# Hybrid attention block: when the branch-weight sums and the pooling weights' high part are issued, and where three down products accumulate

## The chip, the cores and the metric

The kernel runs on one core of one Trainium2 chip. The metric is the device time of one execution in microseconds (us). Before the change the median of 3 runs is 1093.87 us (1093.35 to 1094.19).

## The reference, cut to what matters

One decoder layer on 1024 tokens of width 1024, all in float32 (cut):

```python
h = _rmsnorm(x, g_mix_pre[l])
proj = jnp.einsum('bsd,de->bse', h, w_in[l]) + b_in[l]
u_pool, q, k, v, gates = jnp.split(proj, IN_SPLITS, axis=-1)
y_pool = _multiscale_pool(u_pool, w_pool[l], pool_scale[l])   # 4 groups of 128 channels; w_pool, then * pool_scale
y_attn = _sliding_window_sink_attention(rope(q), rope(k), v, attn_sinks[l])   # 8 heads of 64, window 128, one sink each
g_pool, g_attn = jax.nn.sigmoid(gates)[..., :D_MODEL], jax.nn.sigmoid(gates)[..., D_MODEL:]
merged = (g_pool * jnp.einsum('bsc,cd->bsd', y_pool, w_branch_pool[l])
          + g_attn * jnp.einsum('bsc,cd->bsd', y_attn, w_branch_attn[l]))
x = x + _rmsnorm(jnp.einsum('bsd,de->bse', merged, w_out[l]), g_mix_post[l])
h2 = _rmsnorm(x, g_mlp_pre[l])
ff = jnp.einsum('bsf,fd->bsd',
                jnp.square(jax.nn.relu(jnp.einsum('bsd,df->bsf', h2, w_up[l]))), w_down[l])
x = x + _rmsnorm(ff, g_mlp_post[l])
```

## The kernel before

**Matmuls.** Each float32 operand is split into a high part (a cast, mostly on ScalarE, L101) and a low part (a subtraction, mostly on VectorE, L104), and each product takes three passes on TensorE (PE): high by high, high by low, low by high. The large products are of Strassen's kind, seven products of halves in place of eight, so that sums of weights are formed on VectorE before they are split.

**Attention.** This is the first 150 us or so. The tokens are eight tiles of 128. For a tile, `post_qkv` transposes queries and keys on PE (L345, L346) and splits them. `score_all` forms the scores (matmuls of L389, two groups, each in a PSUM bank tagged `sc`, of which there are two), and ScalarE copies each group to SBUF (L391). `score_prev` puts the previous tile's scores into the masked places on VectorE (L398). `softmax_max` (L405 to L407), `softmax_exp` (ScalarE, L413 for the sinks, then L415 for eight heads) and `softmax_scale` (VectorE: L419 adds the sink to the sum, L420 its reciprocal, L421 scales) follow. `attend_t` transposes the probabilities on PE (L432) and splits them (L101, L104), `attend_own` masks a copy of them (L441), and `attend_v` multiplies by the values on PE and copies the result, `yt`, on ScalarE (L459), out of an `sc` bank. GpSimd (POOL) does beside this the rotation of queries and keys of a tile (L326 to L329) and the copies, differences and splits of its values (L354, L103, L359, L104 with `v`, `dv`, `df`).

The order of PE, VectorE and ScalarE in this stage is written out by hand under `manual_schedule`: each engine issues its instructions in the order of the code. `fill(t)` puts some t us of other matmuls between the steps (L183 is one of their lines): first the query, key and value projections of tiles 4 to 7, closed on VectorE by L312 (queries) and L315 (keys and values), then gate products `half(p, i)` and the four pooling products `wb_mm(gi)`. What these need made ready on ScalarE and VectorE is kept in lists of closures, `between`, `due` and `lazy`, that are flushed at set places; `lazy` behind the scaling L421, or ahead of `wb_mm`.

**The branch sums.** `w_branch_attn` is loaded in two halves h (0 and 1), each into two tiles of the three-buffer pool `st` (tag `st`, `presum_load`, its DMAs at L276 on SP's queue). `presum(h)` is called twice for each: the first call does the sums L286 and L287, the second L282 and L283 and then stores four blocks. All are VectorE additions or subtractions of 128x512 with both operands in SBUF. The loads of half 1 are issued behind the split of the pool weights `wpt` (a ScalarE L101 and a VectorE L104), which also came through a buffer of `st`.

**The pooling weights.** `load_wb(gi)`, called in the stream of `fill` for gi = 3, 2, 1, 0, loads 512 KB of `w_branch_pool` into a buffer of `st` (DMA at L700) and appends one closure `parts`: ScalarE scales it into the high part (L705), VectorE forms the low part (L706). For gi of 3 and 2 it goes to `lazy`, for 1 and 0 to `between`.

**The down stage.** It begins behind the up products and takes the rest of the time. Seven products `PRODUCTS = (1, 5, 2, 3, 6, 7, 4)`, each of eight steps, each step loading and splitting a pair of operands and adding into four PSUM banks [128, 512], one for a tile of 128 tokens (`down_mm`, matmuls L1982). Banks have two tags, `at` and `mm`, of four each. Products 1 and 2 use one set of `at`, 5 and 3 one set of `mm`; 6 takes new `at` banks, 7 new `mm`, 4 new `at`. `u`, `v`, `c11`, `c12` are accumulators in SBUF, four tiles of [128, 512] each. Behind products 1 and 2 ScalarE copies the banks to `u` (L2097) and `c11` (L2101); behind 6, 7 and 4 VectorE adds the banks to `u`, `v` or `c12`. With product 4 the tokens 512 to 1023 are closed tile by tile: in `last_tile` the last six matmul passes of the last tile are done on the left 256 columns, then on the right 256 in a bank of their own, and VectorE adds each to `u` (L2046 whole, L2048 right); the squares, the root, one scaling of the whole `c11` and the output follow.

## Time and profile before

| | |
|---|---|
| median of 3 runs | 1093.87 us (1093.35 to 1094.19) |
| the profiled execution's own time | 1093.78 us |
| its span, first to last instruction | 1092.0 us |
| mean granted TensorE clock | 0.998 of full |
| PE, VectorE, ScalarE, POOL busy | 99%, 74%, 56%, 8% of the span |

All durations are of the one profiled execution; about 1.8 us of its time lies outside the span. In a row of the timeline stand the start, from the span's beginning, and the length in us, the engine (PE, DVE for VectorE, ACT for ScalarE, POOL, SPq for SP's queue of DMAs), the line of the kernel, the operation and its output and inputs; in square brackets the idle time ahead of it and what ended that. "x18" counts instructions that are shown together. A row of the busy times by stretch holds the stretch, its length, then the busy time and the count of instructions of PE, PEld (weight load), DVE, ACT and POOL, then the granted clock, the DMA engines' share and GB/s. A row of DMA transfers ends with the size of one and the median time from issue to landing.

### The profile page before, as it was taken

How to read it: one execution, taken by the hardware profiler on the slowest of the kernel's cores; microseconds unless marked ns; L12 is line 12 of the kernel's file. 1: busy time of each engine (PE TensorE's matmuls, PEld its weight loads, DVE VectorE, ACT ScalarE, POOL GpSimd, SP SyncE). 2: the span in 40 equal slices, each digit the busy share in tenths (PEclk: the TensorE clock that was granted, in tenths of full speed). 3: DMA queues.
4: the chain of work that ended last, by engine and by line, in shares of the span. 5: the costliest groups of instructions: out<-in, count | busy, mean ns of one | idle time of the engine just before them, and what ended most of it. 6: DMA issues, size and time to landing. Idle time of an engine off the chain costs nothing.

```text
span 1092.0 us, 13883 instructions
## 1 busy us (share of the span) xinstructions
PE 1082.5 (99%) x5066; PEld 899.1 (82%) x5066; DVE 810.4 (74%) x1111; ACT 610.8 (56%) x1001; POOL 84.2 (8%) x142
## 2 busy tenths in 40 slices
PE   9999999999999999999999999999999999999997
PEld 8888888888888888888888888888888888888886
DVE  6689888999797887889867665655457866557685
ACT  7557886466654257457665564555346535435461
POOL 0344311100100012100000000000000000000000
PEclk9999999999999999999999999999999999999999
DMA  9858899679865776732565535345697886632622
GB/s 337 189 142 212 212 247 349 189 242 319 255 214 173 225 182 154 270 117 81 180 212 212 193 125 191 127 161 186 223 389 278 298 261 194 195 117 78 212 77 77
DMA packets 98612, 221.02 MB, mean 202 GB/s; under 512 B 10224, under 2 KB 27760, under 8 KB 98544
## 3 DMA queue, kind: packets, MB, share of 16 engines
q1 hardware_dynamic: 82256, 183.56, 50.2%
q0 software_dynamic: 10528, 16.78, 8.6%
q10 hardware_dynamic: 5760, 19.79, 4.8%
q8 instruction: 39, 0.64, 0.2%
q14 instruction: 29, 0.24, 0.1%
HBM read 158.24 MB, written 60.82 MB: 201 GB/s over the span
## 4 chain that ended last, share of the span: by engine, by line
PE 95%; DVE 2%; ACT 2%; DMA 0%; issue 0%; DVEq 0%; ACTq 0%; SPq 0%
PE mm L584 26%; PE at L584 18%; PE at L1982 15%; PE mm L1982 12%; PE mm L1516 5%; PE mm L495 3%; PE sc L183 2%; PE at L1244 2%; PE at L1516 2%; PE mm L192 2%; PE mm L1244 1%; PE mm L183 1%; PE mm L497 1%; PE sc L457 1%; PE sc L389 1%; PE at L1562 1%
## 5 line engine op out<-in xcount | busy, mean ns | idle before, releaser
L1982 PE MATMUL at<-ar,wh 128*128 128x512 f32 x696 | 159.0, 389 | 0.0
L1982 PEld LDWEIGHTS at<-ar,wh 128*128 128x128 f32 x696 | 130.6, 188 | 27.5 <-DVE ar L104 0.4
L1982 PE MATMUL mm<-ar,wh 128*128 128x512 f32 x576 | 131.0, 389 | 0.0
L1982 PEld LDWEIGHTS mm<-ar,wh 128*128 128x128 f32 x576 | 108.1, 188 | 22.5
L104 DVE TENSOR_TENSOR wh<-raw,wh 128x1024 fp32r<-128x1024 f32 x50 | 61.1, 1223 | 68.4 <-ACT wh L101 68.2
L101 ACT CAST wh<-raw 128x1024 fp32r<-128x1024 f32 x50 | 52.6, 1052 | 104.0 <-PE at L1982 51.6
L104 DVE TENSOR_TENSOR wh<-st,wh 128x512 fp32r<-128x512 f32 (+1 forms) x103 | 74.8, 736 | 30.0 <-ACT wh L101 25.5
L584 PE MATMUL mm<-T,wx 128*128 128x512 f32 x375 | 90.4, 389 | 0.0
L584 PEld LDWEIGHTS mm<-T,wx 128*128 128x128 f32 x375 | 70.4, 188 | 14.6
L584 PE MATMUL mm<-gr,wh 128*128 128x512 f32 x321 | 77.2, 391 | 0.0
L101 ACT CAST wh<-st 128x512 fp32r<-128x512 f32 (+2 forms) x102 | 65.7, 653 | 19.3 <-PE at L584 5.6
L584 PEld LDWEIGHTS mm<-gr,wh 128*128 128x128 f32 x321 | 59.9, 188 | 12.2
L584 PE MATMUL mm<-T,wh 128*128 128x512 f32 x267 | 66.1, 389 | 0.0
L104 DVE TENSOR_TENSOR ar<-B,ar 128x1024 fp32r<-128x1024 f32 x43 | 52.5, 1220 | 9.8 <-ACT ar L101 9.4
L584 PE MATMUL at<-gr,wh 128*128 128x512 f32 x243 | 59.0, 389 | 0.0
L584 PE MATMUL mm<-x,wh 128*128 128x512 f32 x240 | 58.9, 394 | 0.0
L584 PEld LDWEIGHTS mm<-T,wh 128*128 128x128 f32 x267 | 50.1, 188 | 10.4
L584 PEld LDWEIGHTS at<-gr,wh 128*128 128x128 f32 x243 | 45.6, 188 | 9.5
L584 PEld LDWEIGHTS mm<-x,wh 128*128 128x128 f32 x240 | 44.2, 188 | 9.6 <-ACT f L693 0.2
L584 PE MATMUL at<-T,wx 128*128 128x512 f32 x213 | 52.0, 389 | 0.0
L101 ACT CAST ar<-B 128x1024 fp32r<-128x1024 f32 x43 | 45.1, 1050 | 12.2 <-DMA B<-in_w_dn_dram 9.4
L584 PEld LDWEIGHTS at<-T,wx 128*128 128x128 f32 x213 | 40.0, 188 | 8.3
(510 smaller groups left out, 2127.0 us busy)
## 6 DMA issues: line engine op xcount, KB each, us to landing
raw<-f_dram SPq DMA_DIRECT2D x52, 512.0 KB, 3.9
B<-in_w_dn_dram SPq DMA_DIRECT2D x32, 512.0 KB, 6.7
f_dram<-g SPq DMA_DIRECT2D x28, 512.0 KB, 3.3
st<-in_w_up_dram SPq DMA_DIRECT2D x24, 512.0 KB, 4.7
g<-spill_dram SPq DMA_DIRECT2D x17, 512.0 KB, 5.7
f_dram<-g ACTq DMA_DIRECT2D x17, 512.0 KB, 2.6
st<-in_w_g_dram SPq DMA_DIRECT2D x16, 512.0 KB, 4.9
g<-in_w_up_dram SPq DMA_DIRECT2D x15, 512.0 KB, 5.9
```

Of the source, the lines that this page charges most:

```text
L101: act.copy(hi, src)
L104: eng.tensor_tensor(lo, src, f32(hi), ALU.subtract)
L183: pe.matmul(bq, xs_[k][n // 4][:, xh, n % 4 * P:(n % 4 + 1) * P], wq[k][:, h, :], start=k == 0 and j == 0, stop=k == NK - 1 and j == 2)
L192: pe.matmul(bkv_of(n), xs_[k][n // 4][:, xh, n % 4 * P:(n % 4 + 1) * P], wkv[k // 2][:, h, k % 2, :], start=k == 0 and j == 0 and not (joi ...
L389: pe.matmul(sb[:, kv, i, :nk], qt[r, qx, m * P:(m + 1) * P], kx[r, k0:k0 + nk], start=j == 0, stop=j == 2)
L457: pe.matmul(yb[:, kv], v[:, c:c + P], p[ph][:, 4 * kv:4 * kv + 4].rearrange("p i q -> p (i q)"), start=j < 2, stop=j >= len(mms) - 2)
L495: pe.matmul(bs[th], whi[:, k, :], rhs(k, hl, th), start=k == 0 and hl == 0, stop=False)
L497: pe.matmul(bs[th], wlo[:, k, :], rhs(k, 0, th), start=False, stop=k == nk - 1)
L584: pe.matmul(b, w[wh][:, kt, :], x_, start=not after and kt == 0 and j == 0, stop=kt == 3 and j == 2, skip_group_check=after)
L1244: pe.matmul(b, w[wh][:, kt, :], xo[xh][:, kt, :], start=not after and kt == 0 and j == 0, stop=kt == 1 and j == 2, skip_group_check=after)
L1516: pe.matmul(bs[t], Am[a][k][ah][:, t * P:(t + 1) * P], Wm[w][k][wh], start=not after and k == 0 and j == 0, stop=k == 3 and j == 2, skip_g ...
L1982: pe.matmul(bs[t], fo[fh][:, k2, t * P:(t + 1) * P], wo_[wh][:, k2, :], start=not after and s2 == 0 and k2 == 0 and j == 0, stop=(s2, k2) ...
```

## The change

Four things are done; no matmul of the attention stage is moved.

1. `presum(0)`'s second call, with L282 and L283 and the four stores, goes from ahead of `softmax_scale(0)` to behind `post_qkv(1)`. Both calls of `presum(1)` go from behind `score_all(2)` and `softmax_max(2)` to behind `attend_t(0)`, which is ahead of `softmax_scale(1)`.
2. The pooling weights' parts become two closures. The one of the high part of gi 3 and 2 is put into a new list `eager`, which is flushed behind each `attend_t`, so ahead of the next tile's exponentials. The low part stays where it was.
3. In the down stage `u` is copied by ScalarE back into the `at` banks behind product 2, and products 6, 7 and 4 add to these. ScalarE copies the banks to `u` behind 6 and 7 for the sums with `c12` and `v`; the closing steps of product 4 read the banks. The squares and scaling of `c12` are issued behind step 0 of product 7.
4. `last_tile` does the right columns first; ScalarE copies the right half of the bank out and VectorE adds the right product to it (256 wide); the left half is read from the bank. `c11` is scaled in two halves.

```diff
@@ -667,7 +667,7 @@
     wu, wb = {}, {}
 
 
-    between, hurry, due, lazy = ([], []), [False], ([], []), []
+    between, hurry, due, lazy, eager = ([], []), [False], ([], []), [], []
 
     def flush(todo):
         while todo:
@@ -699,12 +699,19 @@
         ws = stage([D])
         nc.sync.dma_start(ws, w_bp[gi])
 
-        def parts():
-            hi, lo = wb[gi] = wslot([D]), wslot([D])
-            sc = vec[:, V_PS + gi:V_PS + gi + 1]
-            act.activation(hi, ws, AF.Identity, scale=sc)
-            dve.scalar_tensor_tensor(lo, ws, sc, f32(hi), ALU.mult, ALU.subtract)
-        (lazy if gi > 1 else between[0]).append(parts)
+        sc = vec[:, V_PS + gi:V_PS + gi + 1]
+
+        def high():
+            wb[gi] = wslot([D]), wslot([D])
+            act.activation(wb[gi][0], ws, AF.Identity, scale=sc)
+
+        def low():
+            if gi not in wb:
+                high()
+            dve.scalar_tensor_tensor(wb[gi][1], ws, sc, f32(wb[gi][0]), ALU.mult, ALU.subtract)
+        if gi > 1:
+            eager.append(lambda: gi in wb or high())
+        (lazy if gi > 1 else between[0]).append(low)
 
     def wb_mm(gi):
 
@@ -913,6 +920,7 @@
         softmax_max(0)
         fill(1.7)
         post_qkv(1)
+        presum(0)
         fill(0.7)
         softmax_exp(0, range(3))
         fill(2.5)
@@ -921,7 +929,6 @@
         score_prev(1, 0)
         score_prev(1, 1)
         fill(0.7)
-        presum(0)
         softmax_scale(0)
         post_qkv(2)
         softmax_max(1)
@@ -934,7 +941,11 @@
         fill(3.7)
         for n in range(NT):
             attend_t(n)
+            flush(eager)
             attend_own(n)
+            if n == 0:
+                presum(1)
+                presum(1)
             flush(due[0])
             if n + 1 < NT:
                 early = 1.0 if n > 2 else 0.0
@@ -961,8 +972,6 @@
             hurry[0] = False
             if n + 2 < NT:
                 score_all(n + 2)
-                if n == 0:
-                    presum(1)
                 score_prev(n + 2, 0)
                 score_prev(n + 2, 1)
             flush(due[1])
@@ -976,8 +985,6 @@
                 gt.load(17, yy.tile([P, NK, P], F32, tag="y", name="r17"))
             if n + 2 < NT:
                 softmax_max(n + 2)
-            if n == 0:
-                presum(1)
             if n:
                 attend_sum(n - 1)
         gt.sums56(8)
@@ -2035,23 +2042,27 @@
         t = n - 4
         sums = small(2, "sq")
         b2 = bank("mm", [256])
-        for h, o in ((0, b[:, :256]), (1, b2)):
-            c = slice(h * 256, (h + 1) * 256)
+        left, right = slice(0, 256), slice(256, 512)
+        for o, c in ((b2, right), (b[:, left], left)):
             for s2, k2, _ in order:
                 fo, wo_ = opers[i, s2]
                 for j, (fh, wh) in enumerate(PASSES):
                     pe.matmul(o, fo[fh][:, k2, t * P:(t + 1) * P], wo_[wh][:, k2, c],
-                              start=h == 1 and k2 == 0 and j == 0, stop=k2 == 1 and j == 2, skip_group_check=h == 0)
-            if h == 0:
-                dve.tensor_tensor(u[t], u[t], b, ALU.add)
+                              start=c is right and k2 == 0 and j == 0, stop=k2 == 1 and j == 2,
+                              skip_group_check=c is left)
+            if c is right:
+                r_ = u[t][:, c]
+                act.copy(r_, b[:, c])
+                dve.tensor_tensor(r_, r_, b2, ALU.add)
+                act.activation(junk[:, c], r_, AF.Square, scale=ROOT_D, accum_out=sums[:, 0:1])
+                dve.scalar_tensor_tensor(c11[t][:, c], r_, -0.5, gfin_b[:, c], ALU.mult, ALU.mult)
             else:
-                dve.tensor_tensor(u[t][:, c], u[t][:, c], b2, ALU.add)
-            act.activation(junk[:, c], u[t][:, c], AF.Square, scale=ROOT_D, accum_out=sums[:, h:h + 1])
+                act.activation(junk[:, c], o, AF.Square, scale=ROOT_D, accum_out=sums[:, 1:2])
         e = small()[:, :1]
         dve.tensor_tensor(e, sq[:, 1, n:n + 1], sums[:, 0:1], ALU.add)
         s, ms, r, t2 = (small()[:, :1] for _ in range(4))
         act.activation(s, sums[:, 1:2], AF.Sqrt, bias=e)
-        dve.scalar_tensor_tensor(c11[t], u[t], -0.5, gfin_b[:, :512], ALU.mult, ALU.mult)
+        dve.scalar_tensor_tensor(c11[t][:, left], b[:, left], -0.5, gfin_b[:, left], ALU.mult, ALU.mult)
         dve.tensor_tensor(ms, sums[:, 1:2], e, ALU.add)
         dve.reciprocal(r, s)
         dve.scalar_tensor_tensor(t2, r, r, ms, ALU.mult, ALU.mult)
@@ -2077,39 +2088,47 @@
     for j, (i, s_) in enumerate(steps):
         if j + AHEAD < len(steps):
             operands(*steps[j + AHEAD])
-        if s_ == 0 and i not in (2, 3):
-            tag = "mm" if i in (5, 7) else "at"
-            banks[i] = [bank(tag) for _ in range(4)]
-        bs = banks[{2: 1, 3: 5}.get(i, i)]
+        if s_ == 0 and i in (1, 5):
+            banks[i] = [bank("mm" if i == 5 else "at") for _ in range(4)]
+        bs = banks[{2: 1, 3: 5, 7: 6, 4: 6}.get(i, i)]
         if i == 5:
             square_x1(s_)
         if i == 7 and 1 <= s_ <= 4:
             fin_out(s_ - 1, (c11, c12))
         if i != 4 or s_ < NS - LATE:
-            down_mm(i, s_, bs, i in (2, 3), [(s_, k2, t) for k2 in range(2) for t in range(4)
+            down_mm(i, s_, bs, i not in (1, 5), [(s_, k2, t) for k2 in range(2) for t in range(4)
                                              if (i, s_, t) != (4, NS - LATE - 1, 3)])
+            if (i, s_) == (7, 0):
+                with tc.issue_after(copied.ins):
+                    for t in range(4):
+                        fin_sq(t, 1, c12[t])
+                for t in range(4):
+                    fin_gain(1, c12[t], c12[t])
+                add_eps(slice(0, 4), 1)
+                rsqrt_sum(rr[:, 0:4], sq[:, 0, 0:4], sq[:, 1, 0:4], 4)
             if s_ < NS - 1:
                 continue
         elif s_ < NS - 1:
             continue
+        if i in (1, 6, 7):
+            for t in range(4):
+                copied = act.copy(u[t], bs[t])
         for t in range(4):
             if i == 1:
-                act.copy(u[t], bs[t])
-            elif i == 5:
+                continue
+            if i == 5:
                 act.copy(v[t], bs[t])
             elif i == 2:
                 act.copy(c11[t], bs[t])
+                banks.setdefault(6, []).append(bank("at"))
+                act.copy(banks[6][t], u[t])
                 fin_half(t, 0, c11[t])
             elif i == 3:
                 act.copy(c12[t], bs[t])
             elif i == 6:
-                dve.tensor_tensor(u[t], u[t], bs[t], ALU.add)
                 dve.tensor_tensor(c12[t], c12[t], u[t], ALU.add)
+            elif i == 7:
                 dve.tensor_tensor(v[t], v[t], u[t], ALU.add)
-                fin_half(t, 1, c12[t])
-            elif i == 7:
-                dve.tensor_tensor(v[t], v[t], bs[t], ALU.add)
-                dve.tensor_tensor(u[t], u[t], bs[t], ALU.add)
                 fin_sq(4 + t, 1, v[t])
                 if t == 3:
                     dve.scalar_tensor_tensor(v[t], v[t], -0.5, gfin_b[:, 512:], ALU.mult, ALU.mult)
@@ -2119,15 +2138,14 @@
                 n = 4 + t
                 late = [(s2, k2, t2) for s2, t2 in LATE_ORDER[t] for k2 in range(2)]
                 if t == 3:
-                    down_mm(i, s_, bs, False, late[:-2], late[-3])
+                    down_mm(i, s_, bs, True, late[:-2], late[-3])
                     with tc.manual_schedule(engines={mybir.EngineType.PE, mybir.EngineType.DVE,
                                                      mybir.EngineType.Activation}):
                         last_tile(i, n, bs[t], late[-2:])
                     continue
-                down_mm(i, s_, bs, False, late)
-                dve.tensor_tensor(u[t], u[t], bs[t], ALU.add)
-                fin_sq(n, 0, u[t])
-                fin_gain(0, c11[t], u[t])
+                down_mm(i, s_, bs, True, late)
+                fin_sq(n, 0, bs[t])
+                fin_gain(0, c11[t], bs[t])
                 rsqrt_sum(rr[:, n:n + 1], sq[:, 0, n:n + 1], sq[:, 1, n:n + 1])
                 fin_out(n, (c11, v))
         if i == 2:
@@ -2136,9 +2154,6 @@
             add_eps(slice(4, NT), 1)
             for n in range(4, NT):
                 load_x1(n)
-        if i == 6:
-            add_eps(slice(0, 4), 1)
-            rsqrt_sum(rr[:, 0:4], sq[:, 0, 0:4], sq[:, 1, 0:4], 4)
```

VectorE's order at the first place, from the splits of tile 1 (`qt`, `klo`) to the first step of tile 0's softmax scaling (L419), before (a row holds the line, the operation, output and inputs by the program's names, and the output's size; `st` are the branch weights, `sc` the score banks, `mm` the projections' banks):

```order
L104 TENSOR_TENSOR qt_656<-mm_649,qt_656 128x512
L104 TENSOR_TENSOR klo_471<-mm_650,khi_470 128x128
L312 SCALAR_TENSOR_TENSOR qkv_689<-mm_597,r_86,bc_461 128x512
L398 COPY_PREDICATED s_103_697<-cst,sc_698 128x2x256
L398 COPY_PREDICATED s_103_697<-cst,sc_712 128x2x256
L282 TENSOR_TENSOR st_464<-st_465,st_464 128x512
L283 TENSOR_TENSOR st_465<-st_465,st_464 128x512
L419 TENSOR_TENSOR den_636<-den_636,es_635 128x8
```

The same place after the change:

```order
L104 TENSOR_TENSOR qt_656<-mm_649,qt_656 128x512
L104 TENSOR_TENSOR klo_471<-mm_650,khi_470 128x128
L282 TENSOR_TENSOR st_464<-st_465,st_464 128x512
L283 TENSOR_TENSOR st_465<-st_465,st_464 128x512
L312 SCALAR_TENSOR_TENSOR qkv_695<-mm_597,r_86,bc_461 128x512
L398 COPY_PREDICATED s_103_703<-cst,sc_704 128x2x256
L398 COPY_PREDICATED s_103_703<-cst,sc_718 128x2x256
L419 TENSOR_TENSOR den_636<-den_636,es_635 128x8
```

The pair L282, L283 has passed three instructions, and L419 follows L398 directly.

VectorE's order at the second place, from the split of tile 0's probabilities (L104 of `sc_822`) to the first L398 of tile 2, before:

```order
L104 TENSOR_TENSOR s_122_821<-sc_822,s_121_820 128x1024
L419 TENSOR_TENSOR den_774<-den_774,es_773 128x8
L420 RECIPROCAL den_774<-den_774 128x8
L421 TENSOR_TENSOR s_103_697<-s_103_697,den_774 128x1024
L312 SCALAR_TENSOR_TENSOR qkv_860<-mm_810,r_86,bc_461 128x512
L315 SCALAR_TENSOR_TENSOR qkv_860<-mm_862,r_86,bc_461 128x256
L286 TENSOR_TENSOR st_784<-st_783,st_784 128x512
L287 TENSOR_TENSOR st_783<-st_783 128x512
L398 COPY_PREDICATED s_130_906<-cst,sc_907 128x2x256
```

The same place after the change:

```order
L104 TENSOR_TENSOR s_122_821<-sc_822,s_121_820 128x1024
L286 TENSOR_TENSOR st_784<-st_783,st_784 128x512
L287 TENSOR_TENSOR st_783<-st_783 128x512
L282 TENSOR_TENSOR st_783<-st_784,st_783 128x512
L283 TENSOR_TENSOR st_784<-st_784,st_783 128x512
L419 TENSOR_TENSOR den_774<-den_774,es_773 128x8
L420 RECIPROCAL den_774<-den_774 128x8
L421 TENSOR_TENSOR s_103_703<-s_103_703,den_774 128x1024
L312 SCALAR_TENSOR_TENSOR qkv_868<-mm_810,r_86,bc_461 128x512
L315 SCALAR_TENSOR_TENSOR qkv_868<-mm_870,r_86,bc_461 128x256
L398 COPY_PREDICATED s_130_914<-cst,sc_915 128x2x256
```

All four sums of half 1 now stand ahead of tile 1's softmax scaling; before, two stood behind it and two behind tile 2's first maximum (L407).

ScalarE's order around the first pooling weights, from the cast of tile 2's probabilities (L101 of `sc_1162`) to the copy of its attention output (L459), before:

```order
L101 CAST s_175_1160<-sc_1162 128x1024
L413 ACTIVATE es_1153<-es_1153 128x8
L415 ACTIVATE s_159_1085,den_1154<-s_159_1085,nmx_1152 128x128 x8
L705 ACTIVATE wh_1189<-st_1078,vec 128x1024
L693 COPY f_157_1080<-mm_1081 128x512
L101 CAST wh_1207<-st_1076 128x512
L693 COPY f_157_1080<-mm_1200 128x512
L459 COPY yt_1228<-sc_1229 128x1024
```

The same place after the change, where the high part is at L706:

```order
L101 CAST s_175_1160<-sc_1162 128x1024
L706 ACTIVATE wh_1173<-st_1078,vec 128x1024
L413 ACTIVATE es_1153<-es_1153 128x8
L415 ACTIVATE s_159_1085,den_1154<-s_159_1085,nmx_1152 128x128 x8
L693 COPY f_157_1080<-mm_1081 128x512
L101 CAST wh_1207<-st_1076 128x512
L693 COPY f_157_1080<-mm_1200 128x512
L459 COPY yt_1228<-sc_1229 128x1024
```

The high part has passed the nine exponentials of tile 3.

## The prediction

> **What bounds the kernel now.** I read the page's first part, the busy times by stretch, TensorE's waits and timeline, and then what releases each of those waits. The page, and two stretches (busy time of PE, PEld, DVE, ACT, POOL):
>
> ```profile
> PE 1082.5 (99%) x5066; PEld 899.1 (82%) x5066; DVE 810.4 (74%) x1111; ACT 610.8 (56%) x1001; POOL 84.2 (8%) x142
> ...
> 60.00:80.00 20.00, 19.22 (x125) 16.16 (x125) 16.80 (x30) 10.79 (x36) 7.21 (x14) 1.00 0.52 139
> ...
> 780.00:960.00 180.00, 180.00 (x794) 148.74 (x793) 118.17 (x107) 87.86 (x108) 0.00 (x0) 1.00 0.77 262
> ```
>
> PE is busy 1082.5 of 1092.0 us and has no gap in the down products. So work taken off VectorE or ScalarE there buys nothing. Only PE's few waits in attention, and the stretch behind its last matmul, can be won. PE's timeline has these waits (idle time before a row in brackets), and the chain gives the pace of its matmuls:
>
> ```profile
> 60.55 2.23 PE L183 MATMUL mm<-wh,x 128*128 128x512 f32 x9
> 63.43 1.06 PE L432 MATMUL sc<-cst,s 128*128 128x128 f32 x8 [0.66 <-DVE s L421]
> ...
> 75.60 1.09 PE L432 MATMUL sc<-cst,s 128*128 128x128 f32 x8
> ...
> 100.14 0.39 PE L389 MATMUL sc<-klo,qt 64*128 64x256 f32 x2 [0.33 <-ACT yt L459]
> ```
>
> ```profile
> 76.69 4.12 PE mm L183 x18
> ```
>
> At 4.12/18 = 0.229 us a matmul, the nine from 60.55 would let the transposes L432 start at 62.6, not 63.43: 0.8 us lost. The stretch 60 to 80 lacks 0.78 us, 0.66 of it here, so 0.12 is lost at 75.60. At 100.14 it is 0.33. All the attention edits can win is about 1.25 us.
>
> **First pair of sums, L282 and L283, into the gap before L312.** VectorE now, then POOL (GpSimd) beside it:
>
> ```profile
> 53.26 0.28 DVE L407 TENSOR_TENSOR es<-snk,nmx 128x8 f32<-128x8 f32 x1
> ...
> 55.59 0.75 DVE L312 SCALAR_TENSOR_TENSOR qkv<-mm,r,bc 128x512 f32<-128x512 f32 x1 [1.25 <-PE mm L183]
> 57.40 1.46 DVE L398 COPY_PREDICATED s<-cst,sc 128x512 f32<-128x512 uint32 x2 [1.05 <-ACT s L391]
> 58.75 2.09 DVE L282 TENSOR_TENSOR st<-st,st 128x512 f32<-128x512 f32 x1
> ...
> 62.06 1.23 DVE L421 TENSOR_TENSOR s<-s,den 128x1024 f32<-128x1024 f32 x1
> ...
> 65.44 0.17 DVE L407 TENSOR_TENSOR es<-snk,nmx 128x8 f32<-128x8 f32 x1
> 66.56 0.69 DVE L104 TENSOR_TENSOR wpt<-st,wpt 128x512 fp32r<-128x512 f32 x1 [0.94 <-ACT wpt L101]
> ...
> 70.65 0.17 DVE L419 TENSOR_TENSOR den<-den,es 128x8 f32<-128x8 f32 x1 [1.88 <-ACT s L415]
> ...
> 73.29 0.68 DVE L286 TENSOR_TENSOR st<-st,st 128x512 f32<-128x512 f32 x1
> 74.00 0.89 DVE L287 TENSOR_TENSOR st<-st 128x512 f32<-128x512 f32 x1
> 74.82 1.35 DVE L398 COPY_PREDICATED s<-cst,sc 128x512 f32<-128x512 uint32 x2
> ...
> 78.41 0.69 DVE L282 TENSOR_TENSOR st<-st,st 128x512 f32<-128x512 f32 x1
> ```
>
> ```profile
> 53.16 0.35 POOL L329 TENSOR_TENSOR tf<-tf,rb 128x80 f32<-128x80 f32 x1
> ...
> 53.90 0.53 POOL L327 TENSOR_TENSOR rb<-qkv,cst 128x160 f32<-128x160 f32 x1
> 54.39 0.46 POOL L359 TENSOR_TENSOR df<-vf,vf 128x128 f32<-128x128 f32 x1
> ...
> 59.83 0.46 POOL L104 TENSOR_TENSOR dv<-df,dv 128x128 fp32r<-128x128 f32 x1
> 60.37 0.79 POOL L359 TENSOR_TENSOR df<-vf,vf 128x128 f32<-128x128 f32 x1
> ```
>
> L282 takes 0.69 undisturbed and 2.09 at 58.75: it stood for 1.40 us, until POOL's chain of copies and differences paused at 60.29 (59.83 + 0.46; the next starts at 60.37), and ended 0.55 later, at 60.84. POOL's L359, held by it, ended 0.32 after that (60.37 + 0.79 = 61.16). L407 at 53.26 took 0.28 instead of 0.17: it got in right behind the rotation L329, which ended at 53.51. So rotations (L326 to L329) let VectorE in at their end; the chain of copies and differences does so only where it pauses.
>
> The Trainium skill, page "SBUF — State Buffer", section "Who interferes with whom", says that a VectorE instruction with two SBUF inputs contends with a GpSimd one that reads SBUF, and that the second to issue blocks until the first has finished. The rows agree that it blocks, but L282 waited through five POOL instructions, not one; by the rule my sum below would be 1094.6, by the rows 1095.2.
>
> From 54.34 (55.59 less 1.25) VectorE is free. L282 now waits for L327 (ends at 54.43) and ends at 55.0; L283 gets in behind one of the two rotations left and ends by 56.2; L312 by 56.9; L398 starts at 57.40 as before. No cost there. But each hold delays POOL: L359 ends at 54.98 + 0.32 = 55.30 instead of 54.85, 0.45 late, two holds 0.9. POOL's pause moves to 61.2, and the small sum L419 of the softmax, also with two SBUF inputs, now stands where L282 stood. The reciprocal follows, then the scaling L421, which waits for POOL's last L359 (about 61.27 + 0.46 = 61.73) and ends 1.09 later (1.23 less the 0.14 that such an instruction needs before it reads: 0.69 less 0.55) at 62.8, not 63.29. PE starts at 62.95: 0.45 gained of 0.8. Bounds: 0.8 (L419 isn't held) and a loss (rival D).
>
> **Second set, four sums ahead of the second softmax scaling.** They need loads that wait for a stage buffer, which the wpt split (L104) frees. SP's queue, and the time to landing of these two:
>
> ```profile
> 67.28 0.88 SPq L276 DMA_DIRECT2D st<-in_w_ba_dram  x2
> ```
>
> ```profile
> st<-in_w_ba_dram SPq DMA_DIRECT2D x2, 256.0 KB, 2.9
> ```
>
> The split ends at 67.25 now, and the loads start 0.03 later. With the scaling 0.45 earlier, L407 stands at 65.0 and the split right behind it (its own load comes earlier, being queued behind the first sums' stores): 65.07 to 65.76. Loads at 65.8 and 66.24, the second landing at 69.1. VectorE idles for it, with the softmax scaling queued behind. The four sums take 0.7 + 0.9 + 0.7 + 0.7 = 3.0, so L419 starts at 72.1 instead of 70.65. From L419 to the end of L315 it was 2.64 (70.65 to 73.29): L398 at 74.75, half of its 1.35 later 75.4, PE at 75.5. That is 0.05 to 0.1 before 75.60: the 0.45 is given back, because a DMA now ends last. I take 0.05. Bounds: landing 0.4 sooner gains 0.4; no gain at all loses nothing more than 0.2. The 1.4 us of VectorE freed at 78.41 end no wait of PE.
>
> **The pooling weights' high part ahead of the exponentials.** ScalarE now, SP's issue of the weights, and their landing:
>
> ```profile
> 90.56 1.03 ACT L101 CAST s<-sc 128x1024 fp32r<-128x1024 f32 x1
> 93.38 0.21 ACT L413 ACTIVATE es<-es 128x8 f32<-128x8 f32 x1 [1.78 <-DVE es L407]
> ...
> 96.58 1.14 ACT L705 ACTIVATE wh<-st,vec 128x1024 fp32r<-128x1024 f32 x1
> 97.62 0.56 ACT L693 COPY f<-mm 128x512 f32<-128x512 f32 x1
> ...
> 99.08 1.01 ACT L459 COPY yt<-sc 128x1024 f32<-128x1024 f32 x1
> ```
>
> ```profile
> 89.84 0.34 SPq L700 DMA_DIRECT2D st<-in_w_bp_dram  x1
> ```
>
> ```profile
> st<-in_w_bp_dram SPq DMA_DIRECT2D x1, 512.0 KB, 5.4
> ```
>
> ScalarE idles 1.78 us before 93.38, room for the 1.04 (96.58 to 97.62) of L705. But the weights land at 89.84 + 5.4 = 95.2, and nothing advances this load against PE: it waits for a stage buffer whose last reader follows PE's scores. In ScalarE's order the exponentials of tile 3, two copies, a cast and the copy yt, for which PE waits at 100.14, are queued behind L705. So: 95.2 + 1.04, then 3.20 (93.38 to 96.58), 1.46 (97.62 to 99.08), 1.01 and 0.05 to PE: 101.95, less the 0.05 = 101.9, 1.76 after 100.14. This 1.76 is the state of all the attention edits together, the 0.05 in it. Bounds: a load of 3.8 us costs 0.2, one of 6.5 costs 2.9; I take the row of this very load. The same move for the next weights has its load long landed and moves no wait of PE.
>
> **The down products in one set of banks.** Matmuls, splits and loads keep their number; four copies are added, and adds from PSUM become copies. PE now waits for ScalarE's copy of a bank before product 7 or 4 adds to it. A copy and the cast that may stand ahead of the last:
>
> ```profile
> 908.57 0.59 ACT L2101 COPY c<-at 128x512 f32<-128x512 f32 x1 [1.62 <-PE at L1982]
> ...
> 997.42 1.05 ACT L101 CAST wh<-raw 128x1024 fp32r<-128x1024 f32 x1 [3.43 <-PE at L1982]
> ```
>
> Product 7 starts about 997.6 and reaches the fourth bank nine matmuls later, 999.65. Cast and copy end at about 999.2. Cost nothing, hidden by 0.45; without that cover up to 0.6 at each of two turns.
>
> **The last tile.** Its rows:
>
> ```profile
> 1084.41 0.68 DVE L2046 TENSOR_TENSOR u<-u,at 128x512 f32<-128x512 f32 x1
> ...
> 1085.19 0.42 DVE L2048 TENSOR_TENSOR u<-u,mm 128x256 f32<-128x256 f32 x1
> ```
>
> The 0.68 add goes from the path; a 256-wide product (0.42, like the add) comes onto it behind the last square. 0.68 - 0.42 gives 0.26: I take -0.3, between 0 and -0.68.
>
> **Sum.** +1.76 from the attention (the 0.05 in it) - 0.3 from the last tile = +1.46 on the profiled execution's 1093.78 (0.09 under the median): 1095.2.
>
> **Rivals.**
> B. VectorE waits for one POOL instruction only. The scaling ends before 62.3, PE starts at 62.6, the second set's loads come 0.65 sooner, PE is 0.75 ahead at 75: third cost 1.1, less 0.3, 1094.6. The skill's page named above states this rule. Against: the 2.09.
> C. The load is in time (by 92.3): L705 fills the idle time, yt comes 1.04 sooner, 0.33 gained: -0.05 - 0.33 - 0.3, 1093.1. Against: landing at 95.2.
> D. Slower. L283 misses the last rotation (ends near 56.0) and stands until POOL's pause at 60.75. It ends at 61.3, L312 at 62.0, L398 at 63.3, the scaling at 64.9: PE 1.6 late, 2.05 late after the second set (its chain 2.1 later), then 1.8 more, less 0.3: +3.5, 1097.3. For: the 2.09; against: two rotations are left.
>
> **Numbers.** Forecast 0.62, B 0.18, C 0.08, D 0.12. What a measurement can tell is 0.2%, 2.2 us. The range, 1093.0 to 1096.4, leaves out D and, with 0.07, loads over 6.4 us; it holds C, B and the forecast with all shorter loads. Slower: D and 0.07 from the forecast's upper end, 0.19. Faster: no case reaches 1091.6; 0.03 for what I overlook. Same 0.78.
>
> **What would show it.** Right: L419 near 60.05 long or late; VectorE idle before L286 near 69; ScalarE idle before L706 until its load lands, then PE waiting some 2 us for yt near 100; no wait of PE from 780 on. Wrong: L706 starting before 93, or PE's waits near 63, 75 and 100 all gone.

## The result and the profile after

The changed kernel is slower: the median of 22 executions is 1096.50 us (1094.47 to 1097.96), before 1093.89 (22 executions, 1093.32 to 1095.15); the ratio is 1.0021, 95% interval 1.0015 to 1.0027. The forecast was 1095.2: the sign is right, the 2.61 us are twice the 1.3 that were forecast, and the median lies 0.1 above the upper end of the range. The prediction called 2.2 us what a measurement can tell, and gave a loss beyond that 0.19; it is this case that came, by 0.4 us. The profiled execution took 1096.69 us, 2.91 more than that of before, with a span of 1094.6.

The page's busy times:

```profile
PE 1084.3 (99%) x5066; PEld 901.1 (82%) x5066; DVE 799.0 (73%) x1096; ACT 617.5 (56%) x1014; POOL 81.9 (7%) x142
```

The two stretches of the prediction (busy time of PE, PEld, DVE, ACT, POOL, then the clock):

```profile
60.00:80.00 20.00, 19.59 (x130) 16.81 (x129) 16.81 (x29) 11.45 (x39) 8.12 (x18) 1.00 0.59 180
780.00:960.00 180.00, 180.00 (x795) 149.01 (x795) 116.53 (x106) 92.29 (x114) 0.00 (x0) 1.00 0.77 263
```

VectorE is busy 11 us less and the execution is longer: as before, its mean share says nothing. The stretch from 60 to 80 lacks 0.41 us of PE instead of 0.78, and the down products have no gap. So the loss is elsewhere. PE's timeline of the changed kernel at the prediction's three places:

```profile
63.28 0.93 PE L432 MATMUL sc<-cst,s 128*128 128x128 f32 x7
...
75.73 0.98 PE L432 MATMUL sc<-cst,s 128*128 128x128 f32 x7 [0.41 <-DVE s L398]
...
99.53 0.40 PE L389 MATMUL sc<-khi,qt 64*128 64x256 f32 x4
102.03 0.39 PE L389 MATMUL sc<-klo,qt 64*128 64x256 f32 x2 [2.10 <-ACT yt L459]
...
103.18 1.65 PE L584 MATMUL mm<-x,wh 128*128 128x512 f32 x3
104.62 1.05 PE L345 MATMUL mm<-cst,qkv 128*128 128x128 f32 x4
```

The wait for the copy yt grew from 0.33 to 2.10. Behind it stands what the prediction has no word of: three matmuls of L584 take 1.65 us and four transposes 1.05. Before, they took 0.96 and 0.60:

```profile
101.05 0.96 PE L584 MATMUL mm<-x,wh 128*128 128x512 f32 x3
101.85 0.60 PE L345 MATMUL mm<-cst,qkv 128*128 128x128 f32 x4
```

The granted clock of the changed kernel in the stretches around it (behind the five busy times stands the clock):

```profile
99.00:102.00 3.00, 0.93 (x13) 0.72 (x12) 2.30 (x4) 3.00 (x9) 0.24 (x1) 1.00 0.04 15
102.00:102.50 0.50, 0.47 (x8) 0.47 (x10) 0.50 (x2) 0.50 (x2) 0.00 (x0) 1.00 1.02 410
102.50:106.00 3.50, 3.50 (x20) 2.88 (x17) 2.45 (x4) 1.84 (x4) 0.89 (x1) 0.51 1.01 234
106.00:108.00 2.00, 2.00 (x14) 1.78 (x13) 1.66 (x3) 1.49 (x3) 0.14 (x1) 1.00 0.98 347
```

Some 0.5 us after PE starts again its clock is halved, for 3.4 us (the trace's record of the clock has the changes at 102.58 and 105.99). It runs at full clock ahead of that and behind it. An idle stretch of PE is called a stand from here on.

Both kernels have 5066 matmuls in nearly one order, so the k-th start in one trace can be held against the k-th in the other:

| place | before | after | after is later by | this step |
|---|---|---|---|---|
| 9.9 us, first matmuls | 9.88 | 10.55 | 0.67 | +0.67 |
| transposes L432 of tile 0 | 63.43 | 63.28 | -0.15 | -0.82 |
| transposes L432 of tile 1 | 75.60 | 75.73 | 0.13 | +0.28 |
| second group of L389, tile 4 | 100.14 | 102.03 | 1.89 | +1.76 |
| next matmuls L584 behind the transposes of tile 3 | 103.19 | 106.63 | 3.44 | +1.55 |
| end of the last matmul | 1084.72 | 1087.91 | 3.19 | -0.25 |
| end of VectorE's last L2062, now L2073 | 1088.80 | 1091.44 | 2.64 | -0.55 |
| the whole execution | 1093.78 | 1096.69 | 2.91 | +0.27 |

The first row is no effect of the change, whose first moved instruction comes behind it: the first matmuls run at half pace until the clock comes up, at 5.20 in the trace of before and at 7.00 in that of the changed kernel, and this time differs from one execution to the next (the same row lies from -0.15 to +0.49 in the ten profiles of the experiments). The -0.25 is two slow matmuls at 796.7 in the profile of before, which the changed kernel's has not (0.36 and 0.34 us instead of 0.23). The rest is five effects: -0.82, +0.28, +1.76, +1.55 and, at the end, -0.55 with +0.27 outside the span.

### The profile page after: what moved, and what is told of

Same layout as the page of the kernel before. It is cut to its first block, busy times and chain, and to the rows that moved or that the text cites. A ratio compares the mean times of both kernels' runs of the same rounds, so it can differ in the third digit from the quotient of the medians.

```text
span 1094.6 us, 13878 instructions
## 1 busy us (share of the span) xinstructions
PE 1084.3 (99%) x5066; PEld 901.1 (82%) x5066; DVE 799.0 (73%) x1096; ACT 617.5 (56%) x1014; POOL 81.9 (7%) x142
## 4 chain that ended last, share of the span: by engine, by line
PE 97%; ACT 1%; DVE 1%; DMA 0%; issue 0%; DVEq 0%; ACTq 0%
PE mm L584 26%; PE at L1989 20%; PE at L584 18%; PE mm L1989 8%; PE mm L1523 5%; PE mm L495 3%; PE sc L183 2%; PE mm L192 2%; PE at L1523 2%; PE at L1251 2%; PE mm L183 2%; PE mm L1251 1%; PE mm L497 1%; PE sc L457 1%; PE sc L389 1%; PE at L1569 1%
## 5 line engine op out<-in xcount | busy, mean ns | idle before, releaser
L1989 PE MATMUL at<-ar,wh 128*128 128x512 f32 x888 | 202.1, 389 | 0.0
L1989 PEld LDWEIGHTS at<-ar,wh 128*128 128x128 f32 x888 | 166.7, 188 | 34.6
L104 DVE TENSOR_TENSOR wh<-raw,wh 128x1024 fp32r<-128x1024 f32 x50 | 61.1, 1222 | 70.4 <-ACT wh L101 68.8
L101 ACT CAST wh<-raw 128x1024 fp32r<-128x1024 f32 x50 | 52.7, 1054 | 100.0 <-PE at L1989 63.1
L104 DVE TENSOR_TENSOR wh<-st,wh 128x512 fp32r<-128x512 f32 (+1 forms) x103 | 73.9, 729 | 29.4 <-ACT wh L101 24.9
L584 PE MATMUL mm<-T,wx 128*128 128x512 f32 x375 | 90.4, 389 | 0.0
L1989 PE MATMUL mm<-ar,wh 128*128 128x512 f32 x384 | 87.4, 389 | 0.0
L1989 PEld LDWEIGHTS mm<-ar,wh 128*128 128x128 f32 x384 | 72.1, 188 | 15.0
L584 PEld LDWEIGHTS mm<-T,wx 128*128 128x128 f32 x375 | 70.4, 188 | 14.6
L584 PE MATMUL mm<-gr,wh 128*128 128x512 f32 x321 | 77.2, 391 | 0.0
L101 ACT CAST wh<-st 128x512 fp32r<-128x512 f32 (+2 forms) x102 | 65.7, 653 | 19.2 <-PE at L584 5.5
L584 PEld LDWEIGHTS mm<-gr,wh 128*128 128x128 f32 x321 | 59.9, 188 | 12.2
L584 PE MATMUL mm<-T,wh 128*128 128x512 f32 x267 | 66.1, 389 | 0.0
L584 PE MATMUL mm<-x,wh 128*128 128x512 f32 x240 | 59.5, 397 | 0.0
L104 DVE TENSOR_TENSOR ar<-B,ar 128x1024 fp32r<-128x1024 f32 x43 | 52.4, 1218 | 9.4 <-ACT ar L101 9.0
L584 PE MATMUL at<-gr,wh 128*128 128x512 f32 x243 | 59.0, 389 | 0.0
L584 PEld LDWEIGHTS mm<-T,wh 128*128 128x128 f32 x267 | 50.1, 188 | 10.4
L584 PEld LDWEIGHTS at<-gr,wh 128*128 128x128 f32 x243 | 45.6, 188 | 9.5
L584 PEld LDWEIGHTS mm<-x,wh 128*128 128x128 f32 x240 | 44.5, 189 | 9.7 <-issue 0.2
L584 PE MATMUL at<-T,wx 128*128 128x512 f32 x213 | 52.0, 389 | 0.0
L101 ACT CAST ar<-B 128x1024 fp32r<-128x1024 f32 x43 | 45.2, 1052 | 11.8 <-DMA B<-in_w_dn_dram 9.0
L584 PEld LDWEIGHTS at<-T,wx 128*128 128x128 f32 x213 | 40.0, 188 | 8.3
```

The lines of the kernel that those rows point to most:

```text
L101: act.copy(hi, src)
L104: eng.tensor_tensor(lo, src, f32(hi), ALU.subtract)
L584: pe.matmul(b, w[wh][:, kt, :], x_, start=not after and kt == 0 and j == 0, stop=kt == 3 and j == 2, skip_group_check=after)
L1989: pe.matmul(bs[t], fo[fh][:, k2, t * P:(t + 1) * P], wo_[wh][:, k2, :], start=not after and s2 == 0 and k2 == 0 and j == 0, stop=(s2, k2) ...
```

## The experiments

Theory (late load): the pooling weights land too late for their new place; PE then stands 2 us, and this halves its clock for some 3.4 us in most executions. The moved sums and the last tile give a little. Rivals: the loss comes from the down stage; or the half clock is chance, as at the start, and has nothing to do with the wait.

### One part alone

**The changed kernel with the high part behind the exponentials again.**

```diff
             attend_t(n)
-            flush(eager)
             attend_own(n)
```

> The changed kernel, but the high part of the pooling weights stays behind the exponentials, as before the change (the new list is never flushed). Theory (late load): in the changed kernel the wait for the weights' load costs 1.76 us and, with the 2.1 us that TensorE then stands, half clock for some 3.4 us costs 1.5 more in most executions; the sums moved give 0.55, the last tile 0.6. So here both costs go and both gains stay: 1093.9 - 0.55 - 0.6 = 1092.8, TensorE's wait near 100 at most 0.4 us, no half clock there, executions close together. Rival (down stage): the time is lost behind the matmuls, by the copies and banks or outside the span; then this stays above before, 1094.5 to 1096. Rival (chance): the half clock has nothing to do with the wait and comes by chance; then it is seen here too in more than half of the executions, median near 1094.3.

Measured: 1093.84 (11 executions), before 1093.80 beside it; ratio 1.0003, 0.9992 to 1.0014. Taking this one flush away takes the whole 2.6 us away: the down stage as the place of the loss falls, and so does chance, since ten of eleven executions lie from 1093.07 to 1094.57. (One took 1100.69, at a mean clock of 0.995; what happened in it no profile shows.) But the 1.15 us of gain that the theory left is not there either. VectorE in this kernel's profile:

```profile
60.30 1.22 DVE L419 TENSOR_TENSOR den<-den,es 128x8 f32<-128x8 f32 x1 [1.19 <-ACT s L415]
...
69.64 0.69 DVE L286 TENSOR_TENSOR st<-st,st 128x512 f32<-128x512 f32 x1 [2.07 <-DMA st<-in_w_ba_dram]
```

Here L419, a sum of 128x8, takes 1.22 us. PE gains 0.44 near 63 and loses 0.40 near 75: the prediction's two numbers, 0.45 and all but 0.05 of it.

**The kernel before with that part alone.** The closure of the parts is cut in two and `flush(eager)` added behind `attend_t(n)`, as in the change's diff.

> The kernel before with only the high part of the pooling weights ahead of the exponentials. Theory (late load): TensorE waits some 2.1 us near 100 instead of 0.4, cost 1.76; in most executions half clock for about 3.4 us follows and costs 1.5 more: executions in two groups, near 1095.7 and near 1097.2, median near 1097. Rival (down stage): 1095.7 at most, one group, or less. Rival (chance): one group at 1095.7 with the same spread as before.

Measured: 1097.21, ratio 1.0028 (1.0020 to 1.0037). Four executions lie from 1095.77 to 1095.99, seven from 1097.16 to 1098.36: the two groups, their medians 1.6 us apart. The profile fell in the first:

```profile
95.01 1.15 ACT L706 ACTIVATE wh<-st,vec 128x1024 fp32r<-128x1024 f32 x1 [3.28 <-DMA st<-in_w_bp_dram]
...
101.77 0.39 PE L389 MATMUL sc<-klo,qt 64*128 64x256 f32 x2 [1.80 <-ACT yt L459]
```

ScalarE stands 3.28 us for the load, and PE 1.80 for ScalarE, with no half clock behind it in this execution. The seven are at a mean clock of 0.997, the four at 0.998 or 0.999.

**The moved sums alone, and the down stage alone.** Each is the change's diff of that part, put on the kernel before.

> The kernel before with only the four moved calls of the branch-weight sums. Theory: TensorE's wait near 63 goes (0.83 gained), near 75 it is 0.28 longer since the loads of half 1 land later than the scaling could start; together 0.55 faster, 1093.3. Rival: the 0.83 seen in the changed kernel was of the order of one execution, and the gain is under 0.2.

> The kernel before with only the edits of the down stage (products 6, 7 and 4 in one set of banks, the last tile right columns first). Theory: no wait of TensorE in the down products, and 0.6 less behind the last matmul: 1093.3. Rival (down stage): slower than before by 0.5 to 2 us.

Measured: the sums 1093.92, ratio 1.0004 (0.9994 to 1.0013): no gain, the rival's number, though the profile has -0.78 near 63 and +0.36 near 75. (One execution took 1099.73.) The down stage 1093.59, ratio 0.9998 (0.9989 to 1.0006), 0.2 under before; the profile shows no wait of PE in the down products. The rest of the 0.6 is lost where no row of the trace is: execution less span is 2.0 to 2.15 us on average in each of the six kernels here that have the change's down stage, and 1.78 to 1.85 in before and in the five without it. Where these 0.2 to 0.35 us are spent stays open.

**The first pair of sums alone**, half 1 left where it was.

```diff
         post_qkv(1)
+        presum(0)
         fill(0.7)
...
-        presum(0)
         softmax_scale(0)
```

> The kernel before with only the first pair of sums moved (the second call of half 0 behind the splits of tile 1); half 1 stays where it was. Theory (the load of half 1 gives the gain back): TensorE starts the transposes near 63 earlier by 0.45 or 0.8, by whether VectorE's small sum L419 gets in behind the second POOL instruction or waits for POOL's pause, and the wait near 75 stays at 0.3, since the sums of half 1 stand behind the softmax scaling: 1093.8 - 0.65 = 1093.2. Rival: the gain is given back near 75 all the same (the masked copies wait for the sums of half 1): 1093.8.

Measured: 1093.45, ratio 0.9995 (0.9986 to 1.0004), 0.35 under before and 0.5 under both pairs. Held against before, PE gains 0.3 near 75 in the profile instead of losing 0.36, so by the profiles the give-back near 75 is of the second set. The two medians alone do not show it: they differ by less than their two intervals together. The size (0.65 expected) is smaller, and the profile shows two losses that the expectation has not. PE waited 0.5 us near 56 for the split `klo`, since VectorE had waited for the first sums' load, and POOL's and VectorE's instructions then held each other:

```profile
50.11 1.12 DVE L286 TENSOR_TENSOR st<-st,st 128x512 f32<-128x512 f32 x1 [1.98 <-DMA st<-in_w_ba_dram]
```

Before, this L286 had started at 48.17. And 0.28 is lost again near 85, where PE's load of a weight (PEld) waits for VectorE's split L104, so that three matmuls of L584 take 1.21 us instead of 0.86:

```profile
85.39 0.19 PEld L584 LDWEIGHTS mm<-x,wh 128*128 128x128 f32 x1 [0.52 <-DVE wh L104]
```

This split ended at 83.69 in the profile with both sets moved and ends at 85.34 here, with two sums of half 1 still to do near 78. So the second set loses PE's lead near 75, and without it a part of the lead is lost to VectorE near 85.

### The load

**The changed kernel with the pooling weights' load one place sooner on SP's queue.**

```diff
+            gi = 3 - j // 4
+            if j == 0:
+                load_wb(gi)
             if i == 1:
                 gt.load(2 * steps[j + 4][0])
-            gi = 3 - j // 4
-            if j in (0, 4, 9, 13):
+            if j in (4, 9, 13):
                 load_wb(gi)
```

> The changed kernel with the load of the first pooling weights issued one place sooner on SP's queue, ahead of a load of gate weights (which comes where the pooling weights' load was). Late-load theory: it lands near 81 instead of 95.2, the high part runs in ScalarE's idle time near 92, the exponentials are not held, yt is 1.04 sooner than before the change, TensorE's wait near 100 goes altogether and with it the half clock: 1093.4, 0.4 under the kernel with the high part behind the exponentials. Rival (ScalarE order): the high part ahead of the exponentials costs whether its load is there or not, 1095 or more. Rival (new wait): the gate weights now come late and TensorE waits for their casts: a wait of 1 to 3 us moves to 105 to 115.

Measured: 1093.80 (1093.19 to 1094.63), ratio 1.0001 (0.9992 to 1.0010): 2.7 us less than the changed kernel by the order of two loads alone. ScalarE and PE:

```profile
91.48 1.18 ACT L706 ACTIVATE wh<-st,vec 128x1024 fp32r<-128x1024 f32 x1
...
98.06 1.01 ACT L459 COPY yt<-sc 128x1024 f32<-128x1024 f32 x1
```

```profile
99.67 0.28 PE L389 MATMUL sc<-klo,qt 64*128 64x256 f32 x2
...
102.34 1.09 PE L432 MATMUL sc<-cst,s 128*128 128x128 f32 x8 [0.35 <-DVE s L398]
```

The high part fills the idle time, yt is 1.02 sooner, and the wait near 100 is gone, as the theory had it. The 0.4 are not won: PE waits at the next step, 2.7 us on, for VectorE's masked copies L398, with the low part (1.30 us) ahead of them in VectorE's queue. A new wait, but not the one that the rival named.

### The clock

**The changed kernel with nine matmuls of zeros in the wait.** Ahead of the second group of scores of tile 4, added to a bank of a gate product, which they leave as it was (`last[0]`):

```diff
...
+        if (n, g) == (4, 1):
+            for _ in range(9):
+                pe.matmul(last[0], zeros, zeros.unsqueeze(1).broadcast_to([P, 4, P]), start=False, stop=False,
+                          skip_group_check=True)
         sb = bank("sc", [2, 2, 256])
...
```

> The changed kernel with nine more matmuls of zeros (added to a gate bank that stays as it was, 9 x 0.227 = 2.0 us of work that is thrown away) where TensorE waits for the copy yt near 100. Clock theory: TensorE now stands at most 0.3 us there, the late load still costs its 1.76, but the half clock behind it does not come: no executions near 1097, one group at 1094.5 to 1095.3, median 1094.9, so more work and 1.6 us less than the changed kernel's 1096.5. Rival (chance, or the late load alone): as the changed kernel, two groups, median 1096.5, or 2 us more.

Measured: 1095.53 (1094.71 to 1096.22), ratio 1.0015 (1.0006 to 1.0024). More matmuls, and 1 us less than the changed kernel; executions above 1096.3, twelve of the changed kernel's 22, are gone, and no execution's mean clock is below 0.998. The zeros, and the clock behind them:

```profile
99.42 2.37 PE L385 MATMUL mm<-zeros 128*128 128x512 f32 x9
...
101.72 0.39 PE L393 MATMUL sc<-klo,qt 64*128 64x256 f32 x2
```

```profile
99.00:102.00 3.00, 3.00 (x23) 2.18 (x21) 2.70 (x4) 3.00 (x8) 0.00 (x0) 1.00 0.17 67
102.00:108.00 6.00, 6.00 (x42) 5.04 (x41) 5.81 (x11) 4.28 (x12) 1.03 (x1) 1.00 0.98 302
```

So the half clock came from the stand itself, not from the late load or by chance. The median is 0.6 over the expected 1094.9, and the executions are spread over 1.5 us instead of 0.8; why stays open.

**The kernel before with a longer wait and nothing else**: the copy yt of tile 2 done twice, and done six times.

```diff
-        act.copy(flat(yt), flat(yb))
+        for _ in range(2 if n == 2 else 1):
+            act.copy(flat(yt), flat(yb))
```

> The kernel before with the copy yt of tile 2 done twice, so that TensorE's wait near 100 grows by 0.9, from 0.4 to 1.3 us. Clock theory: too short a stand for the half clock in most executions: 1093.8 + 0.9 = 1094.7, one group. Rival (any longer wait): half clock in half of the executions or more, median 1095.5 or above.

> The kernel before with the copy yt of tile 2 done six times: TensorE stands 0.4 + 5 x 0.9 = 4.9 us near 100. Clock theory: half clock in every execution, for 3.4 us or more, which costs 1.5 to 2: 1093.8 + 4.5 + 1.7 = 1100.0, all executions above 1099.3. Rival (chance): the wait alone, 1098.3.

Measured: twice 1094.71 (1094.23 to 1095.74), as the clock theory had it, one group at a mean clock of 0.998 or 0.999. Six times 1101.06 (1100.65 to 1102.03, five executions at 0.993 to 0.996), 1.1 over the theory. PE's row of each, and the clock of the second:

```profile
101.38 0.39 PE L389 MATMUL sc<-klo,qt 64*128 64x256 f32 x2 [1.38 <-ACT yt L460]
```

```profile
105.77 0.58 PE L389 MATMUL sc<-klo,qt 64*128 64x256 f32 x2 [5.55 <-ACT yt L460]
```

```profile
102.50:105.50 3.00, 0.00 (x0) 0.00 (x0) 0.00 (x0) 2.90 (x4) 0.00 (x0) 0.50 0.47 156
105.50:109.00 3.50, 3.23 (x17) 2.61 (x18) 2.07 (x3) 2.30 (x5) 0.16 (x1) 0.50 0.58 105
109.00:111.00 2.00, 2.00 (x16) 1.88 (x16) 0.86 (x3) 1.25 (x3) 0.87 (x1) 1.00 1.02 219
```

A stand of 1.38 us costs itself. One of 5.55 costs itself and the half clock in every execution; the clock falls while PE still stands, and comes back 3.2 us after it starts again. The copies took longer than the expected 0.9 each, which is part of the 1.1.

**Why only some executions.** The traces' records of the clock answer this for the profiled executions. In all twelve traces of this case every change of the clock lies a whole number of periods of 3.413 us behind the first one, when the clock comes up: 28 in the changed kernel and in the six copies, 317 to 319 for the last one, at the program's end. The first one itself comes at 4.76 to 7.00 us, by execution. So the stand falls differently on these periods (worked out from the clock's records and from PE's rows, in us):

| profile | clock comes up | PE's stand near 100 | idle time by period | half clock from the end of the period |
|---|---|---|---|---|
| copy twice | 6.00 | 100.00 to 101.38 | 1.38 | no |
| high part alone | 5.19 | 99.97 to 101.77 | 0.79, 1.01 | no |
| changed kernel | 7.00 | 99.93 to 102.03 | 2.10 | yes, from 102.58 |
| copy six times | 6.58 | 100.22 to 105.77 | 1.93, 3.41, 0.21 | yes, 102.15 to 108.98 |

Behind the last matmul, too, periods with 1.29 us of idle time or less left the clock full in every trace, and periods with 2.14 or more halved it. By these twelve traces it is the idle time within one period that counts, not the length of the stand: up to 1.38 us did nothing, from 1.93 on the next period ran at half clock. A stand of 1.8 or 2.1 us can lie in one period or across two, which gives one kernel its two groups; for the executions that have no profile this is argued, not shown.

### What helped, together

First pair of sums moved, half 1 as before; the load one place sooner, the high part ahead of the exponentials; its low part behind the masked copies of tile 4; the down stage as changed. Against the changed kernel, beside the load's edit above:

```diff
             attend_own(n)
-            if n == 0:
-                presum(1)
-                presum(1)
...
                 softmax_scale(n + 1)
-                flush(lazy)
+                if n != 2:
+                    flush(lazy)
...
                 score_prev(n + 2, 1)
+                if n == 2:
+                    flush(lazy)
```

The two calls of `presum(1)` stand where they were before the change.

> All that helped together: the first pair of sums moved, half 1 as before the change, the pooling weights' load one place sooner with its high part ahead of the exponentials, its low part (VectorE, 1.3 us) behind the masked copies of tile 4 rather than ahead of them, and the down stage as changed. Theory: 0.65 near 63, the whole wait near 100 (0.35 to 0.45) without the new wait near 102, and 0.25 at the end: 1093.8 - 1.3 = 1092.5, below both kernels. Rival (new wait): the product of the pooling weights near 105 waits for the low part, or the wait near 75 grows: 1093.3 to 1094.

Measured: 1092.65 (1092.41 to 1093.20), ratio to before 0.9989 (0.9981 to 0.9998): 1.15 under before, 3.85 under the changed kernel; 1092.5 was expected. VectorE near 100, and all of PE's waits in this profile that the view lists:

```profile
100.14 1.45 DVE L398 COPY_PREDICATED s<-cst,sc 128x512 f32<-128x512 uint32 x2 [0.17 <-ACT s L391]
101.49 1.27 DVE L711 SCALAR_TENSOR_TENSOR wh<-st,vec,wh 128x1024 fp32r<-128x1024 f32 x1
```

```profile
PE mm L201 <- DVE pad L160: 1.1, 1, 1.1
PE sc L432 <- DVE s L421: 0.2, 1, 0.2
```

The first is at the program's start, in before too. The waits near 75 and 100 are gone; 0.2 near 63 is left. The view lists PE's matmuls alone: the weight load near 85 waits here too, 0.50 us, and PE loses 0.3 by it.

## Why the prediction was right, and where it failed

**First pair of sums.** The mechanism was right to the row. VectorE and POOL of the changed kernel (0.67 late from the start):

```profile
54.93 0.72 DVE L282 TENSOR_TENSOR st<-st,st 128x512 f32<-128x512 f32 x1
55.68 0.83 DVE L283 TENSOR_TENSOR st<-st,st 128x512 f32<-128x512 f32 x1
...
60.71 0.77 DVE L419 TENSOR_TENSOR den<-den,es 128x8 f32<-128x8 f32 x1 [1.20 <-ACT s L415]
...
61.75 1.22 DVE L421 TENSOR_TENSOR s<-s,den 128x1024 f32<-128x1024 f32 x1
...
69.54 0.69 DVE L286 TENSOR_TENSOR st<-st,st 128x512 f32<-128x512 f32 x1 [2.10 <-DMA st<-in_w_ba_dram]
```

```profile
55.06 0.91 POOL L359 TENSOR_TENSOR df<-vf,vf 128x128 f32<-128x128 f32 x1
55.92 0.80 POOL L328 TENSOR_TENSOR qkv<-qkv,rb 128x80 f32<-128x80 f32 x1
...
60.53 0.46 POOL L104 TENSOR_TENSOR v<-vf,v 128x128 fp32r<-128x128 f32 x1
60.93 0.29 POOL L103 CAST dv<-df 128x128 fp32r<-128x128 f32 x1
61.16 0.30 POOL L354 COPY vf<-qkv 128x128 f32<-128x128 f32 x1
61.42 0.47 POOL L104 TENSOR_TENSOR dv<-df,dv 128x128 fp32r<-128x128 f32 x1
```

Neither sum stood long; POOL lost 0.45 twice, the 0.9 of the prediction (0.91 for 0.46, 0.80 for 0.35); and L419 stood where L282 had stood. The step that is too strict is "the chain of copies and differences does so only where it pauses". Here L419 got in at the end of L354 (61.46) and ended at 61.48, so PE gained all of the 0.8; in the kernel with the high part behind the exponentials, with L419 issued at the same place of the same chain, it stood until the pause and PE gained 0.44. Both happen. Rival B's price came out in this profile and in that of the sums alone (L419 took 0.77 there too), its rule did not: L419 stood through the rest of one POOL instruction and two more.

**Second set.** Right: L286 waits 2.10 us for its load with the scaling behind it, and a DMA ends last near 75. The state behind it, -0.05 by the prediction, was -0.55 in this profile (counted from PE's own start), -0.42, -0.16, -0.04 and +0.06 in the four others with both sets moved, and the median of the sums alone is that of before.

**The high part.** Right, and the largest term: L706 was to start at 95.2 when the load lands, with PE at 101.9 to 102.

```profile
95.27 1.15 ACT L706 ACTIVATE wh<-st,vec 128x1024 fp32r<-128x1024 f32 x1 [3.54 <-DMA st<-in_w_bp_dram]
...
100.97 1.01 ACT L459 COPY yt<-sc 128x1024 f32<-128x1024 f32 x1
```

It started at 95.27 and PE at 102.03. That both times agree to 0.1 is in part luck, since PE's late start (+0.67) and its gain in the sums (-0.55 instead of -0.05) all but cancel here; the step itself was 1.76 here and 1.48 in the kernel with this part alone, where 1.81 was forecast (1.76 and the 0.05). Rival C's premise, made true by the earlier load, removes the wait, but its 0.33 is not won: the sum looked at ScalarE alone and VectorE's L398 was next late.

**The step that failed** is the sum itself: "+1.76 from the attention - 0.3 from the last tile" prices a stand of PE at its own length. The 2.1 us stand costs 1.55 more in the matmuls behind it, at half clock. That did not happen in every execution: 8 of the 22 have a mean clock of 0.999 and lie from 1094.47 to 1095.95, median 1094.8; the other 14 have 0.998 (one, at 1097.60) or less and lie from 1095.95 to 1097.96, median 1097.0. Against the eight the forecast is 0.4 too high, against the fourteen 1.8 too low. That it is off from the median by no more than 1.3 is luck, two errors of unlike sign: the attention edits' net was 1.2 in the profile instead of 1.76, and the clock was left out.

**The down products and the last tile.** No wait of PE, as forecast. The last tile, PE and VectorE before:

```profile
1083.84 0.88 PE L2043 MATMUL mm<-hold,hold 128*128 128x256 f32 x6
...
1087.92 0.88 DVE L2062 SCALAR_TENSOR_TENSOR xf<-c,sm,xf 128x256 f32<-128x256 f32 x2
```

and after:

```profile
1087.03 0.88 PE L2050 MATMUL at<-hold,hold 128*128 128x256 f32 x6
...
1088.66 0.42 DVE L2065 SCALAR_TENSOR_TENSOR c<-at,bc 128x256 f32<-128x256 f32 x1 [0.20 <-ACT junk L2060]
...
1090.57 0.87 DVE L2073 SCALAR_TENSOR_TENSOR xf<-c,sm,xf 128x256 f32<-128x256 f32 x2
```

From PE's end to VectorE's end it was 4.08 and is 3.53: 0.55 gained, in the bounds of 0 to 0.68, nearly twice the 0.3 taken. Of this some 0.3 comes back outside the span, for which the prediction has no term, so that the whole is near 0.2.

## What to carry to other kernels

A stand of TensorE of about 2 us can cost more than its length: look up the granted clock behind it, and shorten it or fill it. One profile can miss this, since it comes in some executions only: hold its time against the spread of the others. An instruction moved ahead in an engine's queue needs its input there: move the load first, and then look which engine is next late, since a removed wait is paid only up to the next one. Before sums are moved into an idle stretch, ask which other engine's instructions hold VectorE's there, and whose load now decides.

## What the runs showed of the hardware

- PE's clock fell to 0.50 for 3.41 us after a stand of 2.10 us in the changed kernel's profile. By their times and mean clocks this happened in 14 of its 22 executions, in 7 of 11 of the kernel with the high part alone (a stand of 1.80 in its profile), in none of 11 with a stand of 1.38, and in 5 of 5 with one of 5.55. In the traces the clock changes on a grid of 3.413 us, and it is idle time within one period that halves it: 1.38 did not, 1.93 did. The Trainium skill, page "TensorE: Matmul & The Clock Gate", section "What's actually happening", has a free-running window of about 3.4 us that sets half or full clock; the length of the half clock here, 3.41 us, and that it comes in some executions only, agree. Its section "HAM oscillation — how this bites in real kernels" gives as the rule to avoid gaps over about 3.4 us; here a gap of 2.10 us was enough, and the measurement decides.
- Matmuls of zeros kept the clock up: with nine of them in the gap the profile has full clock, and none of 11 executions a mean clock below 0.998.
- A VectorE instruction with two SBUF inputs can stand through several short POOL instructions, and through three or four from the same place of the same chain: L419, 0.15 to 0.18 us by itself, took 0.77, 1.19 and 1.22.
